# Second block's gate tiles by 2x2 blocks, its convolution summed in PSUM

## The chip, the cores and the metric

One NeuronCore of one Trainium2 chip runs the whole program. The metric is the device time of one execution in microseconds, the median of several runs.

## The reference, cut to what matters

Two blocks on 1024 tokens of width 1024, in float32. The first block is a state-space branch, a sparse attention branch, a merge and a gated feed-forward; it ends in a normalisation. The second block, which the change mostly touches:

```python
h = rmsnorm(x, norm_g); p = h @ w_in                      # 1024 x 8200 columns
gates = sigmoid(p[:, :3072] + b_gate)                     # g_a, g_b, g_c
a = a_in[:, :512] * sigmoid(a_in[:, 512:])                # conformer branch
a = causal_depthwise_conv(a, conv_w, conv_b)              # 31 taps, 512 channels
y_a = (silu(layernorm(a)) * silu(a_z)) @ w_a
y_b = (u * (tril(w_s) @ rmsnorm(v) + b_s) * silu(b_z)) @ w_b   # spatial branch
y_c = (attention(q, k, v, forget gates) * silu(c_z)) @ w_c     # 8 heads of 64
out = x + (g_a * y_a + g_b * y_b + g_c * y_c) @ w_out
```

The feed-forward of the first block is `(silu(u2 @ w_gate) * (u2 @ w_up)) @ w_down` with 2816 hidden columns (22 tiles of 128).

## The kernel before, in words

Activations lie transposed: 128 channels on the partitions, 1024 tokens along a row, eight such tiles for a width of 1024. Each float32 operand is kept as a rounded high half and a remainder, and a product is three matmuls (`mm3`): high x high, high x low, low x high. The halves are made by ScalarE (the cast, L130) and VectorE or GpSimd (the subtraction, L122). `linear` takes a weight 128 output columns at a time: 8 row tiles x 3 passes x 2 token halves = 48 matmuls of 512 columns, after which the caller's `evict` reads PSUM.

`wino` computes a pair of 128-column tiles on both token halves as a 2x2 by 2x2 block product with 7 products in place of 8; each product is 4 row tiles x 3 passes of 512 columns. It needs four sums of weight blocks per pair (`wino_weights`: GpSimd adds, then halves are made) and four sums of activation blocks once (`x4`, tiles `xth`, `xtl`). The weights of the next pair are asked for before the products of the present one. Before the change only the feed-forward uses it: hidden tiles 0 and 1 (pair 0) are computed plainly, and pairs 1 to 10 of gate and up by blocks.

All tiles are placed by a framework that adds the semaphores, hands out SBUF and PSUM, and orders each engine's instructions by a list scheduler with a time model; a manual dependency (`later`, and the third argument of `load`) only orders the schedule. Nearly all DMAs go through SyncE's queue, in order. `self.aside` is a generator of side work; `linear` and `linear_t` take one step of it after each output tile, and `together` sets how many steps that is.

In the order of the program: conditioning rows (`mod_setup`, then `mod_steps`: for each of parts 2, 3 and 4 VectorE sums 8 weighted rows of 1024, and TensorE turns the sum with 8 one-column matmuls directly behind the last row), projections of the first block, state-space branch, sparse attention, `merge1`, `out1` (with part 5 of the conditioning), `ffn`. Then the second block: `conv_in` (inputs of the convolution), `fox` (attention inputs, with `c_z`), `gmlp` (spatial branch), branch b with its 8 gate tiles, `conformer_gate` (`a_z`), the 8 gate tiles of branch c to DRAM, branch a with its 8 gate tiles, attention (`attend`), branch c, `out2`. Beside `fox`, `gmlp` and branch b run `keep_x2` and `conformer`: the convolution, 31 taps per channel tile, even ones on VectorE into an SBUF sum over 1024 tokens (`cx`, L125), odd ones as a ScalarE product and a GpSimd addition (`cy`, L122).

Of the kernel before, what the change touches and what calls it, by code (L numbers as in the profile page):

```python
# [17 lines left out]
T = 1024  # L18
# [50 lines left out]
class Core:  # L69
# [186 lines left out]
    def wino_weights(self, w, c0, kt=8, r0=0):  # L256

        gp, n = self.nc.gpsimd, kt // 2
        raw = self.sb.tile([128, 2 * T], F32, name="wq", tag="wq", bufs=2)[:, :256 * kt].rearrange("p (k n) -> p k n", n=256)
        for k in range(0, kt, n):  # L260
            self.load(raw[:, k:k + n],
                      w[r0 + k * 128:r0 + (k + n) * 128, c0:c0 + 256].rearrange("(k p) n -> p k n", p=128), self.tick)
        a11, a12 = raw[:, :n, :128], raw[:, n:, :128]
        a21, a22 = raw[:, :n, 128:], raw[:, n:, 128:]

        def parts(src, m):
            hi, lo = (blocks(self.pg(t, F32R, bufs=b)[:, :128 * m]) for t, b in (("vh", 4), ("vl", 4)))
            self.split(hi, lo, src)
            return hi, lo
        out = {}  # L270
        h, l = parts(raw[:, :, :128], kt)
        out["a11"], out["a12"] = (h[:, :n], l[:, :n]), (h[:, n:], l[:, n:])
        for name, bufs in (("s12", 1), ("s34", 1)):
            s = blocks(self.pg(name, bufs=bufs)[:, :128 * kt])
            if name == "s12":
                s2, s1 = s[:, :n], s[:, n:]
                self.tt(s1, a21, a22, OP.add, gp)
# [4 lines left out]
            h, l = parts(s, kt)  # L282
# [3 lines left out]
        out["a22"] = parts(a22, n)  # L286
        return out

    def wino(self, jobs, x, weights):
# [10 lines left out]
        def snap(p):  # L300
            if not spare:
                page = blocks(self.pg("snap", bufs=3), 512)
# [5 lines left out]
        for j, (_, evict) in enumerate(jobs):  # L308
# [18 lines left out]
            evict(1, 1, r, u3)  # L327

            def rest(a=a, evict=evict, p=p, r=r, u2=u2):
# [3 lines left out]
                evict(1, 0, p, None)  # L333
        rest()
# [158 lines left out]
    def mod_steps(self, parts):  # L493

        rows = [(part, k) for part in parts for k in range(8)]
        for n in range(0, len(rows), 2):
            for part, k in rows[n:n + 2]:
                w = self.pg("wmod", bufs=4)
                self.load(w, self.mod_rows(part, k), self.pace)
                if k == 0:  # L500
                    acc = self.pg("macc2", bufs=2)
                    self.ts(acc, w, self.cond[:, 0:1])
                else:
                    self.stt(acc, w, self.cond[:, k:k + 1], acc, OP.mult, OP.add)
            yield
            if k == 7:
                p = self.p1()
                for j in range(8):
                    self.mm(p[:, j:j + 1], acc[:, j * 128:(j + 1) * 128], self.ones[:, 0:1])
                self.mod[part] = self.small([8])  # L510
                self.tt(self.mod[part], p[:, 0:8], self.v["b_mod"][:, part * 8:part * 8 + 8], OP.add)
# [604 lines left out]
    def glu(self):  # L1116
# [16 lines left out]
        def ev(m, p):  # L1133
# [7 lines left out]
            self.load(tg, self.tg[i])  # L1141
# [187 lines left out]
    def merge1(self):  # L1329

        w = self.I["w_attn_proj"][0]
        self.mods = self.mod_steps([5])
# [3 lines left out]
        for s in range(2):  # L1336
            c = slice(512 * s, 512 * s + 512)

            def ev(m, p):
# [10 lines left out]
                if s == 1 and m % 2 == 1:  # L1350
# [16 lines left out]
    def out1(self):  # L1367
# [4 lines left out]
        self.stt(gs, self.mod[4], 1.0, self.v["norm2_g"], OP.add, OP.mult)  # L1372
# [12 lines left out]
        def norm(s):  # L1385
            c = slice(512 * s, 512 * s + 512)
            r = self.rsqrt_cols(self.col_sums(acc, half=s), D)
            yield
# [8 lines left out]
            for k in range(4) if s else ():  # L1397
                lo, hi = blocks(self.h[k], 512), blocks(self.h[k + 4], 512)
                b = sh[:, k + 4:k + 5]
                pages = [blocks(self.pg("tq", bufs=3), 512) for _ in range(2)]  # L1400
                (t1, t2), (t3, t4) = ((p[:, 0], p[:, 1]) for p in pages)
                self.tt(t1, lo[:, 1], lo[:, 0], OP.subtract, self.nc.gpsimd)
# [10 lines left out]
        for s in range(2):  # L1413
            c = slice(512 * s, 512 * s + 512)

            def ev(m, p):
# [13 lines left out]
                if s == 0 and m == 1:  # L1430
                    next(self.mods, None)
# [8 lines left out]
    def ffn(self, uh, ul, x4, norm):  # L1440
# [9 lines left out]
        for s in range(2):  # L1450
            c = slice(512 * s, 512 * s + 512)
            th = blocks(self.pg("f_th", bufs=3), 512)

            def ev_g(m, p):
                self.act(th[:, m], p, AF.Tanh, scale=0.5)
                self.stt(th[:, m], th[:, m], 1.0, p, OP.add, OP.mult)
                next(norm, None)

            def ev_u(m, p):
                self.tt(th[:, m], th[:, m], p, OP.mult)  # L1460
                next(norm, None)
            self.linear(wg, cols[:2], 8, uh, ul, ev_g, half=s)
            if s == 1:
                first = self.wino_weights(wg, 256)
            self.linear(wu, cols[:2], 8, uh, ul, ev_u, half=s)
            self.load(fd[0:2, :, c].rearrange("m p t -> p m t"), th)
# [3 lines left out]
        for pair in range(1, 11):  # L1470
# [55 lines left out]
        hl = self.sides("ul", 8)  # L1526
        self.r1 = [None, None]

        def norm(s):
# [10 lines left out]
            for k in range(8):  # L1540
                t = self.pg("sqn", bufs=2)[:, :512]
                self.stt(t, self.h[k][:, c], gg[:, k:k + 1], rb, OP.mult, OP.mult)
                self.split(hh[s][k], hl[s][k], t, eng=self.nc.gpsimd if k % 2 else None)
        norms = [norm(0), norm(1)]
        for s in range(2):
            c = slice(512 * s, 512 * s + 512)

            def ev_last(m, p):
# [3 lines left out]
                self.add_squares(acc2, h, m, fg[:, m:m + 1], half=s)  # L1552
                if s == 1 and m in (1, 3):
# [4 lines left out]
        return hh, hl, norms[1]  # L1558

    def keep_x2(self):  # L1560
# [3 lines left out]
        for k in range(8):  # L1564
            self.ts(self.h[k], self.h[k], fg[:, k:k + 1])
            o = blocks(self.pg("xc", bufs=2))
            for s in range(2):
                q = blocks(self.p1())
                for i in range(4):
                    self.tp(q[:, i], self.h[k][:, (4 * s + i) * 128:(4 * s + i + 1) * 128])  # L1570
# [5 lines left out]
    def fox(self, hh, hl):  # L1576
# [49 lines left out]
        self.fd = self.dram([4, 4, 2, 128, T], "fd")  # L1626
# [58 lines left out]
        for g in range(2):  # L1685
            def ev_v(i, p):
# [4 lines left out]
                self.split(hi, lo, flat(p))  # L1691
# [7 lines left out]
        def ev_z(m, p):  # L1699
            advance()  # L1700
            sz = self.pg("xraw", bufs=5)
            self.mark = self.act(sz, p, AF.Tanh, scale=0.5)
            self.stt(sz, sz, 1.0, p, OP.add, OP.mult)
            self.ts(sz, sz, 0.5, eng=nc.gpsimd)
            self.load(self.fd[m, 3, 0], sz)
        self.linear(w, [(7680 + 128 * t, 128) for t in range(4)], 8, hh, hl, ev_z)
# [59 lines left out]
    def gate(self, hh, hl, j, m, dst):  # L1766
        def ev(_, p):
            self.mark = self.act(dst, p, AF.Tanh, scale=0.5, bias=self.hbg[:, 8 * j + m:8 * j + m + 1])
        self.linear(self.I["w_in_2"][0], [(1024 * j + 128 * m, 128)], 8, hh, hl, ev)

    def branch(self, src, scale, wname, j, hh=None, hl=None):

        w = self.I[wname][0]
        if src is None:
            xh, xl = self.xh, self.xl
# [6 lines left out]
        for m in range(8):  # L1782
            th = self.pg("g_th", bufs=2)
            if hh is None:
                self.load(th, self.gtd[m], self.mark2)
            else:
                self.gate(hh, hl, j, m, th)

            def ev_y(_, p):
                if self.mg[m] is None:  # L1790
                    self.mg[m] = self.pg("mg", bufs=8)
                    self.stt(self.mg[m], th, 1.0, p, OP.add, OP.mult)
                else:
                    self.stt(th, th, 1.0, p, OP.add, OP.mult)
                    self.tt(self.mg[m], self.mg[m], th, OP.add, self.nc.gpsimd)
                if hh is None:
# [5 lines left out]
    def gmlp(self, hh, hl):  # L1802
        nc, I = self.nc, self.I
        w = I["w_in_2"][0]

        ws = self.pg("diag")
        self.load(blocks(ws[:, :512]), I["w_s_2"][0].rearrange("g t s -> t g s"), self.mark)
# [4 lines left out]
        for g in range(4):  # L1812
# [4 lines left out]
                  self.mark)  # L1817
# [49 lines left out]
    def conv_in(self, hh, hl, norm):  # L1867
        w = self.I["w_in_2"][0]
        self.ca = [self.pg("ca", bufs=4) for _ in range(4)]
        self.pace = self.tick  # L1870

        def part(t0, half):
# [7 lines left out]
            def ev_a(m, p):  # L1880
                x = self.ca[t0 + m][:, c]
                self.stt(x, x, 1.0, p, OP.add, OP.mult)
            for c0, ev in ((3584, ev_g), (3072, ev_a)):
# [4 lines left out]

    def conformer(self):

        gp = self.nc.gpsimd
        cw = self.small([31, 4])
        self.ts(cw, blocks(self.v["conv_w_2"], 4), 0.5)
        x = []
        for t in range(4):
            at = self.ca[t]
            y = self.pg("cx", bufs=4)

            self.ts(y, at, cw[:, 30, t:t + 1], self.v["conv_b_2"][:, t:t + 1], OP.mult, OP.add)
            y2 = self.pg("cy", bufs=2)  # L1900
            self.later(gp.memset(y2[:, 0:1], 0.0), self.pace)
            for k in range(29, -1, -1):
                s = 30 - k
                wk = cw[:, k, t:t + 1]
                if k % 2 == 0:
                    i = self.stt(y[:, s:], at[:, :T - s], wk, y[:, s:], OP.mult, OP.add)
                elif s == 1:
                    i = self.act(y2[:, 1:], at[:, :T - 1], scale=wk)
                else:
                    z = self.pg("ct", bufs=2)  # L1910
                    i = self.act(z[:, s:], at[:, :T - s], scale=wk)
                    self.tt(y2[:, s:], y2[:, s:], z[:, s:], OP.add, gp)
                self.later(i, self.pace)
                if k % 4 == 0:
                    yield
            self.tt(y, y, y2, OP.add)
            x.append(y)
            if t == 1:
                total = self.pg("sqa", bufs=4)
            if t > 0:  # L1920
# [157 lines left out]
```

## Time and profile before

| | |
|---|---|
| median of 3 runs | 2697.72 us (2697.37 to 2699.09) |
| the profiled execution | 2699.37 us, span 2697.31 us |
| mean granted TensorE clock | 0.977 |
| TensorE, VectorE, ScalarE, GpSimd busy | 95%, 59%, 41%, 37% |
| second block | from about 1600 us on |

Engines in the rows: PE is TensorE's matmuls, PEld its weight loads, DVE VectorE, ACT ScalarE, POOL GpSimd, SP SyncE; a "q" is an engine's instruction queue. Tiles are named `out<-in`: `wh`, `wl` are a weight's halves, `vh`, `vl` those of a block weight, `uh`, `ul` those of the activations, `pw`, `pl`, `p` PSUM tiles. L159 is every matmul, L135 every load.

### The profile page before, as it was taken

Reading aid. Unit: us, or ns where it says so; the run is one execution under the profiler, and the core shown is the slowest. Engines: PE = TensorE matmul, PEld = TensorE weight load, DVE = VectorE, ACT = ScalarE, POOL = GpSimd, SP = SyncE. Lnnn points to the kernel's source line nnn. Section 1 sums busy time; section 2 is a strip of 40 time slices with the busy share of each in tenths; the row PEclk is TensorE's granted clock in tenths of the full one; section 3 lists DMA queues with packets and bytes.
Section 4 is the critical chain, followed back from the end, with each engine's and each line's share of the span. In section 5 each row is a group of like instructions: output and inputs, shape, how many; then the busy total and the mean of one; then the engine's idle time right before and its main releaser. Section 6 shows DMA issues by size and latency. Waiting matters only on the chain.

```text
span 2697.3 us, 34931 instructions
## 1 busy us (share of the span) xinstructions
PE 2556.0 (95%) x12969; PEld 2152.9 (80%) x12969; DVE 1590.6 (59%) x2626; ACT 1099.2 (41%) x2056; POOL 1011.2 (37%) x931
## 2 busy tenths in 40 slices
PE   6989988896899999999999999999999999999999
PEld 4867877775788778888888888998987888888877
DVE  6753477969884764444453375457589621228871
ACT  6223358685953433333332243344434322118730
POOL 2777642265610264444300031237566210115530
PEclk9989999997999999999999999999999999999999
DMA  7554453464365322222452223344011213238632
GB/s 249 154 196 146 127 153 116 144 208 101 87 231 168 117 67 82 87 86 69 178 182 71 71 87 117 110 157 139 26 39 47 63 36 98 63 84 195 168 115 89
DMA packets 269305, 318.40 MB, mean 118 GB/s; under 512 B 42860, under 2 KB 219704, under 8 KB 269136
## 3 DMA queue, kind: packets, MB, share of 16 engines
q1 hardware_dynamic: 267760, 314.94, 37.9%
q0 software_dynamic: 1152, 1.21, 0.3%
q8 instruction: 102, 1.67, 0.2%
q14 instruction: 67, 0.55, 0.1%
q10 hardware_dynamic: 224, 0.03, 0.0%
HBM read 240.63 MB, written 73.40 MB: 116 GB/s over the span
## 4 chain that ended last, share of the span: by engine, by line
PE 54%; DVE 4%; issue 3%; POOL 2%; DMA 1%; ACT 1%; SPq 0%; DVEq 0%; POOLq 0%; ACTq 0%
PE pl L159 26%; PE pw L159 14%; PE p L159 12%; PE p L167 1%; DVE wl L122 1%; POOL cy L122 1%; DVE cx L125 1%; POOL gv L119 0%; DMA f_th<-fd 0%; DVE bb L122 0%; DMA fvs<-fd 0%; DMA kl<-fd 0%; DVE h L119 0%; DMA wr<-in_w_out_dram 0%; DVE bb L125 0%
## 5 line engine op out<-in xcount | busy, mean ns | idle before, releaser
L159 PE MATMUL pl<-uh,wl 128*128 128x512 f32 x1056 | 415.3, 394 | 6.6 <-DVE wl L122 3.8
L159 PE MATMUL pl<-uh,wh 128*128 128x512 f32 x1056 | 416.2, 395 | 1.7 <-ACT uh L132 1.1
L159 PE MATMUL pl<-ul,wh 128*128 128x512 f32 x1056 | 414.0, 392 | 0.0
L122 DVE TENSOR_TENSOR wl<-wr,wh 128x512 fp32r<-128x512 f32 (+1 forms) x292 | 243.6, 865 | 112.5 <-ACT wh L130 107.7
L130 ACT CAST wh<-wr 128x512 fp32r<-128x512 f32 x340 | 188.3, 596 | 212.5 <-PE pl L159 120.0
L159 PEld LDWEIGHTS pl<-uh,wl 128*128 128x128 f32 x1056 | 199.9, 189 | 49.4 <-DVE wl L122 5.2
L159 PEld LDWEIGHTS pl<-uh,wh 128*128 128x128 f32 x1056 | 200.3, 190 | 42.7 <-ACT uh L132 1.6
L159 PEld LDWEIGHTS pl<-ul,wh 128*128 128x128 f32 x1056 | 200.0, 189 | 41.1 <-DVE ul L125 0.3
L122 POOL TENSOR_TENSOR cy<-cy,ct 128x1021 f32<-128x1021 f32 (+13 forms) x56 | 159.2, 2843 | 79.2 <-ACT ct L132 76.6
L122 POOL TENSOR_TENSOR sqa<-sqa,sqn 128x512 f32<-128x512 f32 (+1 forms) x19 | 29.5, 1568 | 342.7 <-ACT sqn L132 342.7
L159 PE MATMUL p<-wth,uh 128*128 128x256 f32 x512 | 146.1, 286 | 0.0
L159 PE MATMUL p<-wtl,uh 128*128 128x256 f32 x512 | 144.8, 283 | 0.0
L159 PE MATMUL p<-wth,ul 128*128 128x256 f32 x512 | 144.8, 283 | 0.0
L122 DVE TENSOR_TENSOR snap<-pw,snap 128x512 f32<-128x512 f32 x60 | 41.2, 690 | 162.5 <-PE pw L159 87.3
L125 DVE SCALAR_TENSOR_TENSOR cx<-ca,small,cx 128x1022 f32<-128x1022 f32 (+14 forms) x60 | 131.2, 2186 | 1.0
L119 POOL TENSOR_SCALAR L<-L,small 128x128 f32<-128x128 f32 (+7 forms) x128 | 97.9, 771 | 85.6 <-DVE small L1173 80.6
L122 POOL TENSOR_TENSOR mg<-mg,g_th 128x1024 f32<-128x1024 f32 x16 | 47.2, 2955 | 218.1 <-DVE g_th L125 204.5
L159 PE MATMUL pw<-xtl,vh 128*128 128x512 f32 x320 | 124.5, 389 | 0.0
L159 PE MATMUL pw<-xth,vh 128*128 128x512 f32 x320 | 123.7, 389 | 0.0
L159 PE MATMUL pw<-xth,vl 128*128 128x512 f32 x320 | 123.5, 389 | 0.0
L122 POOL TENSOR_TENSOR wl<-wr,wh 128x512 fp32r<-128x512 f32 x48 | 64.5, 1357 | 128.9 <-ACT wh L130 50.9
L122 POOL TENSOR_TENSOR s<-wq 128x512 f32<-128x512 f32 x40 | 59.7, 1494 | 141.0 <-DMA wq<-in_w_ffn_gate_dram 53.6
(443 smaller groups left out, 6966.7 us busy)
## 6 DMA issues: line engine op xcount, KB each, us to landing
wr<-in_w_in_dram SPq DMA_DIRECT2D x64, 512.0 KB, 4.9
wmod<-in_w_mod_dram SPq DMA_DIRECT2D x48, 512.0 KB, 6.8
wr<-in_w_in_dram SPq DMA_DIRECT2D x67, 256.0 KB, 3.2
wr<-in_w_out_dram SPq DMA_DIRECT2D x24, 512.0 KB, 5.5
fd<-f_th SPq DMA_DIRECT2D x22, 512.0 KB, 4.3
f_th<-fd SPq DMA_DIRECT2D x22, 512.0 KB, 5.5
wq<-in_w_ffn_gate_dram SPq DMA_DIRECT2D x20, 512.0 KB, 5.4
wq<-in_w_ffn_up_dram SPq DMA_DIRECT2D x20, 512.0 KB, 4.9
```

The source lines that it names most:

```text
L119: return (eng or self.nc.vector).tensor_scalar(out=out, in0=a, scalar1=s1, scalar2=s2, op0=op0, **kw)
L122: return (eng or self.nc.vector).tensor_tensor(out=out, in0=a, in1=b, op=op)
L125: return self.nc.vector.scalar_tensor_tensor(out=out, in0=a, scalar=s, in1=b, op0=op0, op1=op1)
L130: return self.nc.scalar.copy(out, a)
L159: self.tick = self.nc.tensor.matmul(out, a, b, start=start, stop=stop, skip_group_check=True)
L167: return self.nc.tensor.transpose(out, a, self.ident[:n, :n])
```

## The change

The 24 gate tiles of the second block go through `wino` and to DRAM (`gates2`); the branches only read them back. Pair 1 of the feed-forward becomes plain. The gates `a_z` and `c_z` are computed ahead of the gate stage and kept in DRAM (`plain_gates`), the normalised stream is kept in DRAM (`hd2`) and reloaded by `keep_x2`, and four upper operand tiles go to DRAM over the gate stage (`upper`, `upper_back`). The convolution sums in PSUM, 512 tokens at a time: channel tiles 0 and 1 beside the gate stage with all taps on VectorE, tiles 2 and 3 beside `fox` with the odd taps on ScalarE and GpSimd as before. Part 4 of the conditioning moves from the first projections to `merge1` and `out1`, and each sum is turned three steps behind its last rows. Some GpSimd work goes to VectorE or ScalarE.

```diff
 def wino_weights(self, w, c0, kt=8, r0=0, ref=None):
-    raw = self.sb.tile([128, 2 * T], F32, name="wq", tag="wq", bufs=2)...
+    raw = [self.pg("wq", bufs=3)... for _ in range(2)]
 def wino(...):                       # snap pages 3 -> 2
     evict(1, 1, r, u3)
+    next(self.aside, None)
...
     evict(1, 0, p, None)
+    next(self.aside, None)
 def mod_steps(self, parts):
-    for n in range(0, len(rows), 2):
+    for n in range(0, len(rows) + 6, 2):
...
+        if n >= 12 and n % 8 == 4:
+            turn(parts[n // 8 - 1])
         yield
-        if k == 7: ...               # 8 matmuls, the sum's turn
-self.aside = self.together((self.mod_steps(range(2, 5)), 1.5))
+self.aside = self.together((self.mod_steps((2, 3)), 1.9))
 def merge1(self):
-    self.mods = self.mod_steps([5])  # a step at s == 1 and m % 2 == 1
+    self.mods = self.mod_steps((4, 5))   # at m % 4 == 3; in out1 at s == 0 and m < 7
 def out1(self):                      # operand sums of the first block
-    self.tt(t1, lo[:, 1], lo[:, 0], OP.subtract, self.nc.gpsimd)
+    self.tt(t1, lo[:, 1], lo[:, 0], OP.subtract)
-    self.split(th, tl, p, eng=self.nc.gpsimd if i else None)
+    self.split(th, tl, p)
 def ffn(...):
+    for pair in range(2):            # pairs 0 and 1 plain, in token halves
-    for pair in range(1, 11):
+    for pair in range(2, 11):        # by blocks
...
+    # norm(1): halves 0..3 of the upper operands to DRAM, then t1..t4 as in out1
 def gates2(self, x4, first):
+    for pair in range(12):
+        def ev(m, s, p, more, ...):
+            if more is not None:
+                self.tt(more, p, more, OP.add)
+            self.act(t, p if more is None else more, AF.Tanh, scale=0.5, bias=b)
+            if (m, s) in ((0, 1), (1, 0)):
+                self.load(self.gtd[2 * pair + m], g[m])
+        jobs.append((lambda pair=pair: self.wino_weights(w, 256 * pair), ev))
+    self.wino(jobs, x4, first)
 def conv(self, t, both):
+    taps = range(30, -1, -2 if both else -1)
+    for h in range(2):
+        acc = self.p1()
+        for n, k in enumerate(taps):
+            if s == 0:
+                i = self.ts(acc, at[:, c0:c0 + 512], wk, bias, OP.mult, OP.add)
+            else:
+                i = self.stt(acc[:, a:], at[...], wk, acc[:, a:], OP.mult, OP.add)
+            # both: two odd taps, ScalarE product and GpSimd addition, every second n
 def branch(self, src, scale, wname, j, last=False):
-    self.gate(hh, hl, j, m, th)      # branches a and b
+    self.load(th, self.gtd[8 * j + m], self.mark2 if last else self.pace)
-    self.tt(self.mg[m], self.mg[m], th, OP.add, self.nc.gpsimd)
+    self.tt(self.mg[m], self.mg[m], th, OP.add)
 def gmlp(self, hh, hl):
-    self.ts(x, x, r[:, i:i + 1], eng=nc.gpsimd)
+    self.act(x, x, scale=r[:, i:i + 1])
 def run(self):
     self.conv_in(hh, hl, norm)
+    first = self.plain_gates(hh, hl, norm)
+    self.aside = self.together(((None for t in range(2) for _ in self.conv(t, False)), 0.75))
+    self.gates2(x4, first)
+    self.upper_back(hh, hl)
+    self.spatial()
+    self.aside = ... conformer, conformer_gate, keep_x2, 1.3
     self.fox(hh, hl); self.gmlp(hh, hl)
-    self.branch(self.bb, 0.5, "w_b_2", 1, hh, hl)
+    self.branch(self.bb, 0.5, "w_b_2", 1)
-    self.conformer_gate(hh, hl); 8 gates of branch c to gtd
+    self.branch((self.abh, self.abl), None, "w_a_2", 0)
```

## Rows read from the trace of the kernel before

**Rows 1.** The page's first part: busy us, share of the span, instructions.
```profile
PE 2556.0 (95%) x12969; PEld 2152.9 (80%) x12969; DVE 1590.6 (59%) x2626; ACT 1099.2 (41%) x2056; POOL 1011.2 (37%) x931
```

**Rows 2.** Windows: stretch, length; us (count) of PE PEld DVE ACT POOL; clock; DMA.
```profile
160.00:180.00 20.00, 8.16 (x31) 7.34 (x30) 9.49 (x10) 2.54 (x4) 16.41 (x22) 0.58 0.73 224
810.00:855.00 45.00, 43.93 (x207) 36.30 (x206) 20.64 (x33) 15.29 (x27) 3.86 (x3) 0.96 0.51 167
905.00:958.00 53.00, 43.61 (x185) 34.07 (x183) 47.08 (x62) 23.47 (x36) 21.88 (x12) 0.97 0.24 76
...
1600.00:1690.00 90.00, 87.48 (x411) 73.02 (x412) 46.52 (x75) 25.00 (x45) 12.65 (x8) 0.98 0.29 88
1690.00:1840.00 150.00, 150.00 (x1250) 149.09 (x1249) 80.63 (x141) 56.77 (x82) 52.05 (x23) 1.00 0.48 152
1840.00:2047.00 207.00, 198.29 (x1075) 170.57 (x1074) 152.96 (x108) 76.70 (x116) 134.08 (x54) 0.99 0.18 50
...
2555.00:2593.00 38.00, 34.37 (x165) 28.00 (x165) 26.33 (x24) 14.29 (x21) 20.10 (x9) 1.00 0.31 109
```

**Rows 3.** The chain that ended last: start us, us, what.
```profile
966.84 369.03 PE pw L159 x1628
1338.88 9.12 DMA f_th<-fd
...
2133.64 287.11 PE pl L159 x1267
```

**Rows 4.** Timelines of SP, DVE and PE, 140 to 190: start, us, what [idle before].
```profile
146.59 0.33 SPq L135 DMA_DIRECT2D rot<-s_E  x1
...
160.72 1.24 SPq L135 DMA_DIRECT2D wmod<-in_w_mod_dram  x2
...
166.58 1.28 DVE L125 SCALAR_TENSOR_TENSOR macc<-wmod,small,macc 128x1024 f32<-128x1024 f32 x1 [21.16 <-DMA wmod<-in_w_mod_dram]
...
172.56 3.54 PE L159 MATMUL p<-small,macc 128*128 128x1 f32 x16 [11.84 <-DVE macc L125]
```

**Rows 5.** Timelines of POOL and DVE around 935, and of DVE at 1616.
```profile
935.38 2.38 POOL L122 TENSOR_TENSOR xtl<-tq,xth 128x1024 fp32r<-128x1024 f32 x1 [15.04 <-issue]
...
935.51 4.49 DVE L122 TENSOR_TENSOR wl<-wr,wh 128x512 fp32r<-128x512 f32 x2
...
1616.12 2.49 DVE L122 TENSOR_TENSOR wl<-wr,wh 128x512 fp32r<-128x512 f32 x4
```

**Rows 6.** Groups by shape, 966:1336, 1600:2430, page: busy, mean ns | idle.
```profile
L122 DVE TENSOR_TENSOR vl<-s,vh 128x1024 fp32r<-128x1024 f32 x39 | 50.8, 1302 | 24.4 <-ACT vh L130 15.4 <-POOL f_th L122 4.7 <-PE pw L159 2.3
L122 DVE TENSOR_TENSOR snap<-pw,snap 128x512 f32<-128x512 f32 x58 | 39.8, 690 | 156.1 <-PE pw L159 85.2 <-ACT snap L130 70.7
...
L122 DVE TENSOR_TENSOR vl<-wq,vh 128x512 fp32r<-128x512 f32 x20 | 20.4, 1022 | 1.9 <-PE pw L159 1.9
...
L122 POOL TENSOR_TENSOR s<-wq 128x512 f32<-128x512 f32 x38 | 56.2, 1482 | 141.0 <-DMA wq<-in_w_ffn_gate_dram 53.6 <-DMA wq<-in_w_ffn_up_dram 46.4 <-PE pw L159 22.0
...
L125 DVE SCALAR_TENSOR_TENSOR cx<-ca,small,cx 128x994 f32<-128x994 f32 x4 | 13.0, 3252 | 0.1
...
L125 DVE SCALAR_TENSOR_TENSOR ca<-ca,p 128x512 f32<-128x512 f32 x8 | 5.5, 684 | 20.3 <-PE p L159 20.3
...
L125 DVE SCALAR_TENSOR_TENSOR cx<-ca,small,cx 128x1022 f32<-128x1022 f32 x4 | 5.1, 1276 | 0.0
...
L122 POOL TENSOR_TENSOR cy<-cy,ct 128x1021 f32<-128x1021 f32 (+13 forms) x56 | 159.2, 2843 | 79.2 <-ACT ct L132 76.6
```

**Rows 7.** Waits of PE, 1330 to 1530: us, times, longest.
```profile
PE pl L159 <- DVE fl L122: 1.2, 1, 1.2
```

**Rows 8.** The chain at the end of the spatial branch: start us, us, what.
```profile
2041.45 2.87 DVE bb L122
...
2044.40 1.06 ACT atth L132
...
2045.49 1.24 DVE attl L125
```

More of the change, by code (lines that the diff above doesn't have):

```diff
@@ L495, in mod_steps, with turn @@
         rows = [(part, k) for part in parts for k in range(8)]
-        for n in range(0, len(rows), 2):
+        sums = {}
+        def turn(part):
+            p = self.p1()
+            for j in range(8):
+                self.mm(p[:, j:j + 1], sums[part][:, j * 128:(j + 1) * 128], self.ones[:, 0:1])
+            self.mod[part] = self.small([8])
+            self.tt(self.mod[part], p[:, 0:8], self.v["b_mod"][:, part * 8:part * 8 + 8], OP.add)
+        for n in range(0, len(rows) + 6, 2):
             for part, k in rows[n:n + 2]:
@@ L1451, in ffn, with ev_g, ev_u @@
             c = slice(512 * s, 512 * s + 512)
[L1452 to L1466, printed above, removed]
+            for pair in range(2):
+                th = blocks(self.pg("f_th", bufs=3), 512)
+                def ev_g(m, p):
+                    self.act(th[:, m], p, AF.Tanh, scale=0.5)
+                    self.stt(th[:, m], th[:, m], 1.0, p, OP.add, OP.mult)
+                    next(norm, None)
+                def ev_u(m, p):
+                    self.tt(th[:, m], th[:, m], p, OP.mult)
+                    next(norm, None)
+                two = cols[2 * pair:2 * pair + 2]
+                self.linear(wg, two, 8, uh, ul, ev_g, half=s)
+                if s == 1 and pair == 1:
+                    first = self.wino_weights(wg, 512, ref=self.tick)
+                self.linear(wu, two, 8, uh, ul, ev_u, half=s)
+                self.load(fd[2 * pair:2 * pair + 2, :, c].rearrange("m p t -> p m t"), th)
         for _ in norm:
@@ L1526, in ffn @@
         hl = self.sides("ul", 8)
+        self.hd2 = self.dram([8, 128, T], "hd2")
+        self.upper = self.dram([2, 4, 128, 512], "upper")
+        x4 = {"t1": [], "t2": [], "t3": [], "t4": []}
+        for name, s, ks in (("b11", 0, range(4)), ("b21", 0, range(4, 8)), ("b22", 1, range(4, 8))):
+            x4[name] = [(hh[s][k], hl[s][k]) for k in ks]
         self.r1 = [None, None]
@@ L1708, in fox_heads, with upper_back @@
+    def upper_back(self, hh, hl):
+        for i, (x, tag) in enumerate(((hh, "uh"), (hl, "ul"))):
+            for k in (0, 2):
+                p = blocks(self.pg(tag, bufs=8), 512)
+                self.load(p, self.upper[i, k:k + 2].rearrange("k p t -> p k t"), self.pace)
+                p = p.bitcast(F32R)
+                x[1][k], x[1][k + 1] = p[:, 0], p[:, 1]
     def fox_heads(self):
@@ L1764, in fox_heads, with branch @@
         yield
[L1766 to L1771, printed above, removed]
+    def branch(self, src, scale, wname, j, last=False):
         w = self.I[wname][0]
-        if src is None:
-            xh, xl = self.xh, self.xl
+        if isinstance(src, tuple):
+            xh, xl = src
         else:
@@ L1882, in ev_a @@
                 self.stt(x, x, 1.0, p, OP.add, OP.mult)
+                if half == 1:
+                    self.load(self.cad[t0 + m], self.ca[t0 + m])
             for c0, ev in ((3584, ev_g), (3072, ev_a)):
@@ L1889, in conformer @@
     def conformer(self):
         gp = self.nc.gpsimd
[L1892 to L1920, printed above, removed]
-                self.tt(total, x[0] if t == 1 else total, y, OP.add, gp)
-            self.show(f"conv{t}", y)
@@ L1923, in conformer @@
+        yield from self.conv(2, True)
+        x = self.cx
+        for t in range(2):
+            x[t] = self.pg("cx", bufs=4)
+            self.load(x[t], self.cyd[t], self.pace)
+        yield from self.conv(3, True)
+        total = self.pg("sqa", bufs=4)
+        self.tt(total, x[0], x[1], OP.add, gp)
+        yield
+        self.tt(total, total, x[2], OP.add, gp)
+        self.tt(total, total, x[3], OP.add)
+        yield
         mean = self.small([8])
```

238 lines of the change are left out of this document (165 added, 73 removed).

## The prediction

> **What bounds the kernel now.** I read the page first: TensorE is busy for 95% of the span, VectorE for 59% [rows 1]. Then the windows by stage, to see which stage has slack on the engines that the change loads [rows 2]. Then the chain of waits, because a busy share of modelled matmuls is no rate: the first block's 2x2-block stage puts 1628 matmuls of 512 columns into 369.03 us, and the second block's gate tiles put 1267 into 287.11 us [rows 3]. Both are 0.2267 us each, so both stages run at one rate without a gap, and a matmul fewer there is 0.2267 us less. Last, what the windows leave idle of TensorE, and what stands on the timeline and the chain there.
>
> The kernel is bound by the number of matmuls in most stages, and by late operands at four places: 11.8 us of 20 at 160 to 180, 53 - 43.61 = 9.4 us before the 2x2-block stage of the first block, 207 - 198.29 = 8.7 us in the spatial branch, 38 - 34.37 = 3.6 us in the last branch [rows 2].
>
> **The change part by part.** The profiled execution took 2699.37 us with a span of 2697.31 us; the median of the runs shown is 2697.72 us, 1.65 us lower. The sum is a difference, so I take it from the median.
>
> *Gate tiles.* A pair of tiles of 128 columns takes 2 x 48 = 96 matmuls plainly, and 7 products x 4 row tiles x 3 passes = 84 by blocks. 12 pairs save 144 x 0.2267 = 32.6 us.
>
> *First block, pair 1.* Gate and up of one pair go back to the plain form: 2 x 12 = 24 matmuls more, +5.4 us. So TensorE's own sum is -27.2 us.
>
> *Conditioning steps.* At 160 to 172 TensorE stood 11.84 us, since its column sums stood in its queue before the last two rows of the weight had been multiplied; VectorE had waited 21.16 us for that load, and the load had gone out at 160.72, behind a table store that SyncE's queue could only pass at 146.59 [rows 4]. The window's granted clock was 0.58, so the stop also ran what followed at 1.2 GHz for part of it [rows 2]. The change asks for the sums three steps behind the last rows, makes more steps per tile (1.9 for 1.5), and takes 8 of the 24 loads out of this stage. It may still meet the same blocked queue: bounds 0 and -14 (the wait and some 2 us of low clock); I take -8. The steps that move go into the two merge stages: 8 rows of 1.28 us on VectorE [rows 4], and 8 loads of 512 KB. In the out-projection's first half VectorE is busy 20.64 of 45 us and DMA at 0.51 [rows 2], so they are covered; were they not, 4 steps x 1.28 x 2 = 10 us. I take 0.
>
> *Start of the first block's 2x2 stage.* From 905 to 958 VectorE is busy 47.08 of 53 us [rows 2], and TensorE stands for 9.4. One reason is in the rows: four weight subtractions of 512 columns take 2.49 us undisturbed, 0.62 each, and two took 4.49 us while GpSimd ran a subtraction of its own from 935.38 [rows 5]. The change moves GpSimd's part to VectorE and has twice the plain tiles (16 half tiles of 24 x 0.2267 = 5.4 us, 87 us) over it. VectorE's work there: the normalisation 16 x 0.68 = 10.9, the operand sums 4 x (0.62 + 3 x 0.68 + 2 x 1.24) = 20.6 (1024 columns taken as twice 512), and weights and evictions 16 x (1.24 + 0.68) = 31: 62 of 87 us. It can bunch in the first half (47 of 43.5 us). Bounds +4 and -10; I take -6.
>
> The Trainium skill (SBUF — State Buffer, Who interferes with whom) says that a VectorE instruction with two SBUF inputs and a GpSimd instruction that reads SBUF take turns at a shared port, and one with at most one SBUF input does not. By that rule all 9.4 us should go, and the sum would be -41.6; the trace agrees in kind, the 4.49 us beside 2 x 0.62, but the bunching is left, and the sum keeps -6.
>
> *Second normalisation and operand sums.* The same work, in the convolution's input stage: VectorE is busy 46.52 of 90 us [rows 2]. What is added is 4 subtractions of 0.62 and 20.6 us of sums, spread over the sixteen half tiles and the first whole ones; what goes is the scaling of the kept activations. Covered; without cover, 3 us. I take 0.
>
> *Inside the gate stage.* New beside 12 x 84 x 0.2267 = 228.5 us of matmuls: VectorE makes five halves per pair (1.30 twice, 1.02 three times at most) and adds three snapshots (0.69 each), 7.7 us, x 12 = 92 us [rows 6]; and the convolution of two channel tiles, 31 taps x 2 halves x 2 = 124 instructions that add 512 columns into PSUM. No row before writes PSUM from VectorE. From below, a 512-column instruction with one PSUM operand is 0.68 us; from above, the present tap of 994 columns in SBUF is 3.25 us beside GpSimd, 1.68 us per 512 columns [rows 6]. At 0.68 the tap work is 84 us and VectorE is busy 176 of 228 us; at 1.68 it is 208 and VectorE needs 300. I take 0.68, the nearest row: same length, one PSUM operand. GpSimd has only 5.8 us per pair of sums there (4 x 1.48) [rows 6]. ScalarE's copies and halves are half a pair's time, as in the first block, where this stage shows no wait. Late operands: +2.
>
> *Into and out of the gate stage.* The block weights are made two tiles (21.8 us) ahead; on leaving, the next projection needs its first weights and the 8 upper operands back from DRAM, with memory that the last products free. The like passage in the first block has a 9.12 us load on the chain [rows 3], of which 1.2 us was left as a wait for its lower half [rows 7]. I take +4, bounds 1 and 13.
>
> *Attention inputs.* Half of the convolution runs beside them: 64 taps x 0.68 = 44 us on VectorE, which is busy 80.63 of 150 us, without the kept rows, and 28 additions of 2.8 us [rows 6] = 80 us on GpSimd, which is busy 52.05 us, some of these additions among it: 132 of 150 us at most [rows 2]. TensorE has no wait there now. One of the four PSUM banks is held by the sum. +2, bounds 0 and 17 (below).
>
> *Spatial branch.* GpSimd is busy 134.08 of 207 us and VectorE 152.96 [rows 2]; the 8.7 us stand behind taps of up to 3.25 us [rows 6] and a product of 2.87 us [rows 8]. Half of the taps are gone, the others mostly done, and the scaling goes from GpSimd to ScalarE. I take -7, bounds 0 and -8.7.
>
> *Branches without gates.* 16 tiles of 24 x 0.2267 = 5.4 us replace tiles of 16.3. VectorE needs 0.62 + 1.24 + 1.24 = 3.1 us per tile. What lacks cover is the start: the last product of the spatial branch, 2.87 at most, its rounding, 1.06, and its lower half, 1.24 [rows 8], stood under a gate tile of 10.9 us; now only three row tiles, 9 matmuls, 2.0 us, go ahead of it: +3. In the last branch the addition moves from GpSimd to VectorE: of the 3.6 us, -1.
>
> Sum: -32.6 + 5.4 - 8 - 6 + 0 + 0 + 2 + 4 + 2 - 7 + 3 - 1 = -38.2 us; 2697.7 - 38.2 = 2659.5, so 2660 us.
>
> **The rivals.**
> *The matmuls alone* (chance 0.23): the waits move rather than go. TensorE's -27.2 us are sure once the stage runs at its rate; the conditioning load stays behind the blocked queue (0), VectorE bunches before the first 2x2 stage (0), the spatial branch keeps half (-4), and entries and starts cost 13: 2697.7 - 27.2 - 4 + 13 = 2680. For it: a wait removed here was one of several late operands. Against: the rows name the cause of two of them.
> *VectorE becomes the bound of the gate stage* (0.08): the place is the 124 PSUM taps. It decides from 92 + 124 t = 228, t = 1.10 us. At 1.68 the stage takes 300 us, +72 on the forecast: 2732, slower. At 1.28, +23: 2683. For it: reading and writing one PSUM range in place, instruction upon instruction, stands in no row. Against: the present taps are in place too, and run at 1.28 us for 1022 columns when undisturbed [rows 6].
> *GpSimd holds the attention inputs* (0.09): GpSimd has up to 132 of 150 us there. A weight half of VectorE that has to wait for one 2.8 us addition in each of the 6 groups costs 17 us: 2677. For it: the present taps, which run beside those additions, go from 1.28 to 3.25 us. Against: the stage had its first additions already, and TensorE stood for nothing.
>
> The rule of the Trainium skill named above is what would do it; the price is worked out from the addition's row.
> *All waits go* (0.12): -27.2 - 14 - 9.4 - 8.7 - 2, and +7 for the new passages: 2643. For it: each has a named cause that the change touches. Against: four things must go right at once.
> *No change to speak of* (0.04): entries and exits each wait for a whole load chain, twice 13 us: 2697.
>
> **How the numbers follow.** The forecast has 0.44, 2650 to 2670. 2660 is its time. The range of 2640 to 2688 takes in the matmuls alone, GpSimd's and the good case, and leaves out VectorE's bound and the rest, 0.15 or so. This measurement tells apart 0.2%, 5.4 us. Slower by more than that: the larger part of VectorE's rival and mishaps, 0.08. Within: 0.05. Faster: 0.87.
>
> **What would show it.** Right: block products of the gates at 0.227 us each, 1008 of them, in under 235 us; taps near 0.68 us; no 11.8 us wait for the conditioning sums; under 5 us of waits before the first 2x2 stage. Wrong: VectorE at nine tenths in the gate stage; TensorE waiting for weight halves beside GpSimd's additions in the attention inputs; waits over 10 us where the gate stage begins or ends.

## The result, and the profile after

The changed kernel takes 2614.59 us, median of 4 runs (2612.61 to 2621.87), beside 2698.40 us for the kernel before; the ratio is 0.9692, 95% interval [0.9672, 0.9713]. That is 83.8 us less; the forecast was 38 less, 2660 us, with a range that ended at 2640. The profiled execution took 2621.87 us with a span of 2620.2 us, so of the 83.8 us the two traces place 77.1; the rest is the distance of this execution to its median and is not placed.

The first part of the page; against [rows 1] TensorE has 120 matmul records less, GpSimd 163 us less to do, VectorE 63 us more.

```profile
PE 2515.9 (96%) x12849; PEld 2119.9 (81%) x12849; DVE 1653.9 (63%) x2882; ACT 1129.7 (43%) x2144; POOL 847.9 (32%) x889
```

Windows of the second block, columns as in [rows 2]: the convolution's input, the gate stage, attention inputs, spatial branch, last branch. The length less PE's busy time is what TensorE stood.

```profile
1541.00:1633.00 92.00, 90.27 (x406) 74.01 (x405) 62.50 (x98) 37.76 (x63) 5.69 (x4) 1.00 0.42 139
...
1720.00:1954.00 234.00, 234.00 (x1056) 194.81 (x1055) 165.14 (x217) 97.56 (x148) 63.41 (x46) 1.00 0.39 128
...
1973.00:2155.00 182.00, 172.20 (x1425) 171.40 (x1424) 116.89 (x175) 80.27 (x131) 101.30 (x43) 0.98 0.34 109
2155.00:2267.00 112.00, 106.87 (x520) 89.88 (x519) 71.14 (x95) 34.33 (x48) 4.77 (x2) 0.97 0.31 94
...
2475.00:2528.00 53.00, 51.82 (x260) 43.48 (x259) 40.41 (x50) 25.45 (x38) 7.58 (x8) 1.00 0.51 189
```

VectorE's groups by shape in and around the gate stage (1715 to 1960): busy us, mean ns of one. The first row is the operation that no row of before showed, a tap that adds 512 columns into PSUM: 0.752 us.

```profile
L125 DVE SCALAR_TENSOR_TENSOR p<-ca,small,p 128x512 f32<-128x512 f32 x60 | 45.1, 752 | 1.2
L122 DVE TENSOR_TENSOR vl<-s,vh 128x1024 fp32r<-128x1024 f32 x22 | 32.2, 1462 | 3.2 <-ACT vh L130 3.0
L122 DVE TENSOR_TENSOR snap<-pw,snap 128x512 f32<-128x512 f32 x36 | 24.8, 690 | 53.8 <-PE pw L159 34.5 <-ACT snap L130 18.9
L122 DVE TENSOR_TENSOR vl<-wq,vh 128x512 fp32r<-128x512 f32 x33 | 21.8, 685 | 1.3 <-ACT vh L130 1.3
```

What TensorE waited for in the attention inputs (us in all, times, longest), and, in the second fence, before the 2x2 stage of the first block, where [rows 2] had 9.4 us:

```profile
PE p L167 <- POOL xraw L122: 5.3, 1, 5.3
PE p L159 <- DVE xsl L125: 3.1, 1, 3.1
PE pl L167 <- DVE small L125: 1.4, 1, 1.4
```

```profile
PE p L159 <- DVE wl L122: 1.4, 1, 1.4
PE p L159 <- ACT wh L130: 0.5, 1, 0.5
```

**Where the time came from.** Two marks cut the program: the merge's first matmul (`p<-atth,wh`) and the second block's first.

| stretch | before | after | difference | forecast |
|---|---|---|---|---|
| start to merge | 759.3 | 712.0 | -47.3 | -8 |
| merge to second block | 829.1 | 829.1 | 0.0 | -0.6 |
| second block | 1108.9 | 1079.1 | -29.8 | -29.6 |

So the large edits came out as forecast, and what was missed lies ahead of the merge, where the diff has only the conditioning steps and one line in `glu`, the output stage of the state-space branch: `self.load(tg, self.tg[i], self.pace)`. It is not among the lines of the change shown above, and the prediction did not price it at all. Ahead of the merge TensorE stood for 104.5 us before and for 66.9 after, and was busy for 9.7 us less, at a mean granted clock of 0.93 before and 0.96 after:

```profile
0.00:759.30 759.30, 654.77 (x3399) 547.40 (x3400) 537.65 (x1213) 418.30 (x936) 402.25 (x521) 0.93 0.49 151
...
0.00:712.00 712.00, 645.10 (x3382) 536.01 (x3383) 534.91 (x1203) 418.04 (x935) 394.07 (x521) 0.96 0.50 156
```

**What ends the stretch before the merge.** Three groups of the timeline by tile, for the kernel before: the state-space branch's products (`s_d`), the keys with which the threshold search of the sparse attention begins (`tk_l`; there are six), and the masks it ends with (`mb`). Each row: minimum, median and longest in ns, then the start of the first and of the last. The last row is the early load of `tg`.

```profile
L159 PE MATMUL p<-s_d,s_O x128: 269/275/582, 293.5 to 457.3; 128*128 128x127 f32 x128
...
L119 DVE TENSOR_SCALAR tk_l<-sc x6: 415/602/1426, 262.8 to 371.0; 128x384 int32<-128x384 int32 x1, 128x512 int32<-128x512 int32 x1, 128x640 int32<-128x640 int32 x1, 128x768 int32<-128x768 int32 x1
...
L119 DVE TENSOR_SCALAR mb<-tk_eq x5: 293/395/2458, 604.3 to 641.2; 128x512 bf16<-128x512 bf16 x1, 128x640 bf16<-128x640 bf16 x1, 128x768 bf16<-128x768 bf16 x1, 128x896 bf16<-128x896 bf16 x1
...
L135 SPq DMA_DIRECT2D g_tg<-tg x2: 338/338/338, 248.3 to 265.9; - x2
```

The same of the changed kernel; its first two `tg` loads go out at 462.59 and 481.37.

```profile
L159 PE MATMUL p<-s_d,s_O x128: 269/275/578, 240.4 to 430.2; 128*128 128x127 f32 x128
...
L119 DVE TENSOR_SCALAR tk_l<-sc x6: 369/586/1248, 272.8 to 289.7; 128x384 int32<-128x384 int32 x1, 128x512 int32<-128x512 int32 x1, 128x640 int32<-128x640 int32 x1, 128x768 int32<-128x768 int32 x1
...
L119 DVE TENSOR_SCALAR mb<-tk_eq x5: 362/733/1514, 521.1 to 556.6; 128x512 bf16<-128x512 bf16 x1, 128x640 bf16<-128x640 bf16 x1, 128x768 bf16<-128x768 bf16 x1, 128x896 bf16<-128x896 bf16 x1
...
462.59 0.39 SPq L135 DMA_DIRECT2D g_tg<-tg  x1
481.37 0.46 SPq L135 DMA_DIRECT2D g_tg<-tg  x1
```

Before, the sixth key came at 371.0 and the last mask at 641.2. VectorE reads the attention's logits out of PSUM only behind their masks, and TensorE stood for it. TensorE's timeline of the kernel before, idle time in brackets, and its window:

```profile
606.34 0.44 PE L159 MATMUL pl<-akh,aqq 128*128 128x384 f32 x1 [3.85 <-DVE small L1169]
618.07 0.80 PE L159 MATMUL pl<-akh,aqq 128*128 128x512 f32 x1 [7.67 <-DVE small L1169]
...
640.72 1.75 PE L167 MATMUL p<-small,L 128*128 128x128 f32 x7 [5.21 <-POOL L L119]
```

```profile
600.00:650.00 50.00, 25.30 (x92) 20.55 (x91) 48.03 (x89) 18.01 (x38) 18.99 (x24) 0.64 0.50 125
```

TensorE is busy half of that window, at a granted clock of 0.64: part of it ran at 1.2 GHz, with VectorE full. After, the window from 600 to 700 is

```profile
600.00:700.00 100.00, 94.37 (x660) 83.45 (x659) 89.02 (x258) 90.74 (x221) 66.81 (x115) 0.98 0.40 96
```

### The profile page after: what moved, and what is told of

The parts are those of the page before. It is cut to its first block, busy times and chain, and to the rows that moved or that the text cites. A ratio compares the mean times of both kernels' runs of the same rounds, so it can differ in the third digit from the quotient of the medians.

```text
span 2620.2 us, 35143 instructions
## 1 busy us (share of the span) xinstructions
PE 2515.9 (96%) x12849; PEld 2119.9 (81%) x12849; DVE 1653.9 (63%) x2882; ACT 1129.7 (43%) x2144; POOL 847.9 (32%) x889
## 5 line engine op out<-in xcount | busy, mean ns | idle before, releaser
L130 ACT CAST wh<-wr 128x512 fp32r<-128x512 f32 (+1 forms) x308 | 170.7, 594 | 325.1 <-PE pl L159 125.9
L159 PE MATMUL pl<-uh,wh 128*128 128x512 f32 x672 | 266.6, 397 | 1.1 <-ACT uh L132 1.1
L159 PE MATMUL pl<-uh,wl 128*128 128x512 f32 x672 | 264.6, 394 | 0.6 <-DVE wl L122 0.6
L159 PE MATMUL pl<-ul,wh 128*128 128x512 f32 x672 | 263.9, 393 | 0.0
L159 PEld LDWEIGHTS pl<-uh,wl 128*128 128x128 f32 x672 | 127.8, 190 | 27.7 <-DVE wl L122 1.1
L159 PEld LDWEIGHTS pl<-uh,wh 128*128 128x128 f32 x672 | 127.6, 190 | 26.9 <-ACT uh L132 1.2
L159 PEld LDWEIGHTS pl<-ul,wh 128*128 128x128 f32 x672 | 127.9, 190 | 26.2 <-DVE ul L125 0.5
L159 PE MATMUL pw<-uh,vh 128*128 128x512 f32 x360 | 140.0, 389 | 0.0
L159 PE MATMUL pw<-ul,vh 128*128 128x512 f32 x360 | 140.0, 389 | 0.0
L159 PE MATMUL pw<-uh,vl 128*128 128x512 f32 x360 | 136.6, 389 | 0.0
```

The costliest lines, as they stand in the source:

```text
L130: return self.nc.scalar.copy(out, a)
L159: self.tick = self.nc.tensor.matmul(out, a, b, start=start, stop=stop, skip_group_check=True)
```

## The experiments

Differences to the changed kernel are between ratios to the kernel before on the same chip, times 2698 us; each ratio's interval is about 0.002 to either side, so one such difference is known to some 7 us.

**Conditioning alone, and undone.** The first theory: the stretch ahead of the merge is the conditioning edits' work. They were put alone into the kernel before, and alone taken out of the changed one.

```diff
 # mod_steps, merge1, out1 and run as in the change; nothing else
-self.aside = self.together((self.mod_steps(range(2, 5)), 1.5))
+self.aside = self.together((self.mod_steps((2, 3)), 1.9))
```

> The kernel before with the conditioning edits alone (part 4 moved to the merge stages, each sum turned three steps late, 1.9 steps per tile). Theory: these edits carry nearly all of what the first block gained, 47 us at the first merge matmul (759.3 to 712.0): 2650 us (2645 to 2662), the threshold search's last counting pass at about 490 us in place of 557, TensorE not idle at the start of the sparse attention. Rival: the edits are worth the one stop of 11.8 us and some low clock, and the rest of the first block's gain comes with the other parts of the change (memory that they free, another order): 2684 to 2690 us, the search still ending near 557.

> The changed kernel with the conditioning as before (parts 2 to 4 in the first projections, turned at once, 1.5 steps per tile, part 5 in the merge). Theory: the first block loses its gain, 2614.6 + 45 = 2660 us (2648 to 2664). Rival: 2614.6 + 8 to 13 = 2623 to 2628 us.

Alone: 2710.23 us, ratio 1.0052 [1.0035, 1.0068], slower by 13 us; both the theory and its rival missed. Undone: 2638.06, ratio 0.9782 [0.9762, 0.9801], 24 us over the changed kernel, between the theories. The same edits cost time in one kernel and save it in the other. In the trace of the run alone, the state-space branch ended earlier than before, yet the last mask came later:

```profile
L159 PE MATMUL p<-s_d,s_O x128: 269/275/582, 240.1 to 448.8; 128*128 128x127 f32 x128
...
L119 DVE TENSOR_SCALAR mb<-tk_eq x5: 293/359/2454, 620.3 to 651.2; 128x512 bf16<-128x512 bf16 x1, 128x640 bf16<-128x640 bf16 x1, 128x768 bf16<-128x768 bf16 x1, 128x896 bf16<-128x896 bf16 x1
```

**Gate tiles plain, and pair 1 by blocks again.** To see whether the steps that looked right were right.

```diff
 def gates2(self, hh, hl):
+    self.linear(w, [(128 * m, 128) for m in range(24)], 8, hh, hl, ev)
-    self.wino(jobs, x4, first)
```

> The changed kernel with the 24 gate tiles computed plainly in the place of the block products, everything else kept (the operand sums for the blocks are made and not used). Theory: 144 matmuls more at 0.2267 us, +32.6 us, and nothing else moves: 2647 us (2643 to 2652). Rival: the block stage lets VectorE or its entries hold it up, so that less than the matmuls is lost by the plain form: +20 us or less, under 2637 us.

2650.48 us, ratio 0.9827 [0.9810, 0.9843]: 36 us over the changed kernel, as the count of matmuls says (32.6).

```diff
-for pair in range(2):      # plain pairs; by blocks from 2
+for pair in range(1):      # plain pair 0; by blocks from 1
```

> The changed kernel with pair 1 of the feed-forward by blocks again, so that the plain cover before the first 2x2-block stage is one pair as in the kernel before. Theory: 24 matmuls fewer, -5.4 us, but the waits for weight halves before the stage come back, +8 us: 2617 us (2612 to 2621), with 6 to 10 us of waits there. Rival: what removed the waits is the move of GpSimd's part to VectorE, and the cover was not needed: 2609 us, under 3 us of waits.

2620.08 us, ratio 0.9715 [0.9700, 0.9729]: 6 us over, inside what can be told, and the two profiled executions lie the other way round (spans of 2617.8 us here, 2620.2 in the changed kernel). Its trace has 4.4 us of waits before the 2x2 stage, not the 6 to 10 of the theory, beside 1.9 in the changed kernel and 9.4 before [rows 2]. So most of the waits went without the longer cover, and whether the 24 matmuls that the plain pair adds are paid back stays open.

**The `tg` line alone, and undone.** The second theory: the early `tg` loads hold two pages of SBUF over the search.

```diff
-self.load(tg, self.tg[i])
+self.load(tg, self.tg[i], self.pace)
```

> The kernel before with one line of the change: the load of the stored gate (g_tg) in the state-space branch's output stage is ordered behind the last output tile, and no longer free to go out as early as the schedule likes. Theory: that early load (248 and 266 us) holds two 4 KB pages for 270 us, the threshold search's last key then has no page until 371, and the sparse attention starts late; so this line alone brings the search's second step from 379 to about 285, its last counting pass from 556 to under 515, and 25 to 40 us: 2665 us (2655 to 2675). Rival: the load is off the path and the first block's gain belongs to the conditioning edits together with the memory that the rest of the change frees: 2690 us or more.

> The changed kernel with that one line as before (g_tg loads free to go early). Theory: the two loads go out near 265, the search's second step comes only at about 390, the sparse attention starts with TensorE idle, and the time is 2614.6 + 50 = 2665 us (2650 to 2675), as the kernel with the conditioning edits alone lost 57 us in the first block against the changed one. Rival: 2614 to 2622 us.

Alone 2680.21 us, ratio 0.9933 [0.9918, 0.9947], -18 us, less than the theory expected and more than the rival. Undone in the changed kernel 2671.71, ratio 0.9900 [0.9885, 0.9915], 56 us over it, as expected. With the line undone the key is late again, as in the kernel before:

```profile
L119 DVE TENSOR_SCALAR tk_l<-sc x6: 494/687/1495, 271.8 to 350.1; 128x384 int32<-128x384 int32 x1, 128x512 int32<-128x512 int32 x1, 128x640 int32<-128x640 int32 x1, 128x768 int32<-128x768 int32 x1
...
L119 DVE TENSOR_SCALAR mb<-tk_eq x5: 295/359/2459, 619.8 to 650.7; 128x512 bf16<-128x512 bf16 x1, 128x640 bf16<-128x640 bf16 x1, 128x768 bf16<-128x768 bf16 x1, 128x896 bf16<-128x896 bf16 x1
```

**Is it the room or the loads?** An early `tg` is two pages, but also two transfers, two places in SyncE's queue and two GpSimd instructions. So two pages, and then one, were held idle in the changed kernel, without the transfers; all that they add is a GpSimd memset and a VectorE read of one column for each page. `tg` itself stays late.

```diff
+self.hold2 = [self.pg("hold2", bufs=2) for _ in range(2)]   # 4 KB a partition each
+for x in self.hold2: nc.gpsimd.memset(x[:, 0:1], 0.0)
...
+    if i < 2:          # read once at the first gate tiles, then free
+        self.later(self.ts(keep[:, i:i + 1], self.hold2[i][:, 0:1], 1.0), self.mark)
```

> The changed kernel with two idle pages of 4 KB kept from the first gate tile of the projections until the first two gates of the output stage, so that SBUF has as little room as with the early loads, but no early load. Theory (room): the search's last key is late again and the time rises by 20 to 55 us, 2635 to 2670 us. Rival (the early loads hurt as transfers, in SyncE's queue or by their bandwidth): 2614 to 2622 us.

> The changed kernel, with one idle page of 4 KB a partition held from the first projections until the first gate tile of the first block; two such pages cost 71 us. If there is just no room to spare, one page costs some part of that: 2630 to 2670 us, with the sixth key of the search between 300 and 370 us. If there is a page to spare, 2611 to 2622. If any page held delays the last key alike, 2675 to 2690.

Two pages: 2685.46 us, ratio 0.9956 [0.9939, 0.9973], 71 us over, more than the 20 to 55 expected. One page: 2638.97, ratio 0.9770 [0.9755, 0.9784], 21 us over, as expected. Two pages held:

```profile
L692 POOL MEMSET hold<- x2: 102/102/102, 11.9 to 11.9; 128x1 f32 x2
L119 DVE TENSOR_SCALAR small<-hold x2: 144/146/148, 519.4 to 534.9; 128x1 f32<-128x1 f32 x2
...
L119 DVE TENSOR_SCALAR tk_l<-sc x6: 352/658/1443, 290.1 to 367.9; 128x384 int32<-128x384 int32 x1, 128x512 int32<-128x512 int32 x1, 128x640 int32<-128x640 int32 x1, 128x768 int32<-128x768 int32 x1
...
L119 DVE TENSOR_SCALAR mb<-tk_eq x5: 294/360/2452, 636.8 to 667.7; 128x512 bf16<-128x512 bf16 x1, 128x640 bf16<-128x640 bf16 x1, 128x768 bf16<-128x768 bf16 x1, 128x896 bf16<-128x896 bf16 x1
```

The pages are written at 11.9 us and read at 519.4 and 534.9, so they are held from long before the early loads take theirs (266.6 and 278.4 with the line undone), and the first key comes 18 us later than with the line undone. From the first key on the two runs are alike: 78 us to the sixth key in both, and 494 and 497 us to the merge, where the changed kernel takes 439. So behind the first key two pages, without the loads, cost what the early loads cost; that the whole is 71 us and not 56 fits the longer hold. The same memsets and reads on a small tile were not tried. Two kernels whose edits come only behind the merge, the plain gates and pair 1 by blocks, reach the merge at 710.8 and 712.2, the changed kernel at 712.0.

One page held: the sixth key comes 27 us later than in the changed kernel, and the state-space branch ends 17.5 us later.

```profile
L159 PE MATMUL p<-s_d,s_O x128: 269/275/578, 255.0 to 447.7; 128*128 128x127 f32 x128
...
L119 DVE TENSOR_SCALAR tk_l<-sc x6: 360/662/1511, 270.7 to 316.7; 128x384 int32<-128x384 int32 x1, 128x512 int32<-128x512 int32 x1, 128x640 int32<-128x640 int32 x1, 128x768 int32<-128x768 int32 x1
```

**Which part of the conditioning edits?** Part 3 moved as well; then, one at a time, the immediate turn, part 4 and the rate as they had been.

```diff
-self.aside = self.together((self.mod_steps((2, 3)), 1.9))
+self.aside = self.together((self.mod_steps((2,)), 1.9))         # part 3 to the merge
+self.aside = self.together((self.mod_steps((2, 3, 4)), 1.9))    # part 4 back
+self.aside = self.together((self.mod_steps((2, 3)), 1.5))       # rate as before
+if k == 7: ...                                                  # turn behind the last row
```

> The changed kernel with part 3 of the conditioning also moved from the first projections to the merge stages (part 2 alone stays). Theory: one part moved out is worth half of what both conditioning edits gave here (23.5 us), since the index scores stand behind the rows in VectorE's queue: 2604 us (2598 to 2612). Rival: no further gain, since the scores already start at 158, or a loss in the merge, whose window already has DMA at 0.84: 2615 to 2625 us.

2611.45 us, ratio 0.9676 [0.9660, 0.9692]: 4 us under the changed kernel, not to be told from it, so the further gain of the theory is not shown. In this run the merge also takes a conditioning step at every second tile, in place of every fourth.

> The changed kernel, with each conditioning sum turned directly behind its last rows again; part 4 stays in the merge, the rate stays 1.9. With all of the conditioning edits undone the kernel took 23.5 us more than the changed one. If the late turn carries that (TensorE no longer stands behind the sum, 11.8 us, and runs at 2.4 GHz behind it), this takes 2628 to 2642 us. If moving part 4 carries it (eight loads and eight rows less before the index scores), this takes 2612 to 2622.

2623.70 us, ratio 0.9714 [0.9700, 0.9729]: 6 us over, inside the noise; its trace reaches the merge at 711.4, as the changed kernel's at 712.0, and TensorE waits 2.0 us for a conditioning sum.

> The changed kernel, with part 4 of the conditioning back in the first projections (parts 2, 3 and 4 there, part 5 in the merge); the late turn and the rate of 1.9 stay. If moving part 4 carries the 23.5 us of the conditioning edits, 2628 to 2642 us and index scores from about 175 us on. If the late turn carries them, 2612 to 2622 and index scores from about 159 us on. Where both are needed, this and the run without the late turn both come out above 2625.

2649.28 us, ratio 0.9802 [0.9786, 0.9818]: 30 us over. The index scores start at 157.6, early, against the 175 expected where the move matters, but TensorE waits 20.8 us in them for ScalarE (`rel`), 4.3 in the changed kernel, and the state-space branch ends at 464.7, later than before. So of the conditioning edits it is mostly the move that pays. That this run is no better than the one with all of them undone fits the late turn's price in room, since a sum's page is then held three steps longer; this was not tried apart, and what the 20.8 us have to do with room is not shown.

> The changed kernel, with the conditioning steps taken at 1.5 per tile, as before, in place of 1.9; the late turn and the move of part 4 stay. If the rate is without effect, 2611 to 2619 us. If the steps must be through early (their pages are wanted by the search's keys), 2622 to 2650, with the sixth key of the threshold search later than 300 us.

2628.25 us, ratio 0.9732 [0.9717, 0.9746]: 11 us over, with the sixth key at 317.0: as the second theory has it.

**What the twelve runs have in common.** The starts fit two chains that race to the merge: the search's masks, and the state-space branch with the first block's gate tiles behind it. Starts of the last `s_d` product, the sixth key, the last mask and the merge, read from each trace by tile:

| kernel | last `s_d` | sixth key | last mask | merge | less mask | less `s_d` |
|---|---|---|---|---|---|---|
| before | 457.3 | 371.0 | 641.2 | 759.3 | 118.1 | 302.0 |
| conditioning alone | 448.8 | 350.9 | 651.2 | 769.1 | 117.9 | 320.3 |
| `tg` undone | 449.1 | 350.1 | 650.7 | 768.4 | 117.7 | 319.3 |
| two pages held | 466.6 | 367.9 | 667.7 | 784.4 | 116.7 | 317.8 |
| `tg` alone | 454.7 | 278.0 | 595.6 | 738.6 | 143.0 | 283.9 |
| conditioning undone | 448.2 | 273.7 | 588.9 | 730.8 | 141.9 | 282.6 |
| part 4 back | 464.7 | 321.0 | 593.5 | 746.7 | 153.2 | 282.0 |
| one page held | 447.7 | 316.7 | 582.8 | 734.3 | 151.5 | 286.6 |
| rate as before | 449.3 | 317.0 | 587.0 | 729.0 | 142.0 | 279.7 |
| after | 430.2 | 289.7 | 556.6 | 712.0 | 155.4 | 281.8 |

Where the key is late (350 or more), the merge starts 117 to 118 us after the last mask, whatever the state-space branch did. Where it is early, 280 to 287 us after the last `s_d` in this table, whatever the masks did. The four runs that the table leaves out lie at 278 to 284 after the last `s_d`. By it the numbers of both edits alone come out: before, the state-space chain was ready at 457.3 + 283 = 740 by this estimate, so freeing the masks alone could bring no more than 19 us, and it brought 20.7 at the merge; the conditioning edits alone brought that chain to 732, but the masks came 10 us later, and so did the merge. Only both together let the merge start at 712. The other parts of the change add less: 0.7 us at the merge between conditioning alone and `tg` undone, 7.8 between `tg` alone and conditioning undone. The rule was seen after the runs, and it is read from traces; which tile of the search waits for which page is in no row, and stays open. The kernel before with both edits and nothing else was not tried.

## Why the prediction was wrong

**The step that failed** is the conditioning steps' -8, with bounds 0 and -14, and with it the `tg` line at nothing. It priced the one wait that the rows named, 11.84 us [rows 4]. That wait was not the price: it is gone from the changed kernel, and with the turn immediate again but part 4 moved it is 2.0 us, and nothing is lost that can be measured. What the edits did, as the runs with held pages and with the old rate have it, is give pages back while the search starts: the early `tg` loads held two from 248 us on, and part 4's rows, loaded until 187 us, and its sum, turned at 266, some more before. That it is pages for the conditioning rows too is argued from these runs; no run holds pages in their place. Worth, in the changed kernel: 56 us for the `tg` line, 24 us for conditioning, and 47 for the whole change at the merge, not their sum, since each needs the other. The place to see it in the trace of before was there: a window of 50 us with TensorE half busy, and behind it a last mask whose key came at 371 where four of the six had come by 270 us. I had listed four places of late operands and not this one, the largest. Freed alone it is worth 19 us by the table, and it brought 20.7 at the merge; the rest is mostly the interaction, for which both chains had to be followed.

**Gate tiles, -32.6**: right; plain gates gave 36 back. The stage's 234 us show no wait and hold the 1008 block products and 48 narrower matmuls of the next stage, VectorE at 165 of 234 (176 of 228 forecast), a tap at 0.752 us (0.68 taken, 1.68 the upper bound). The rival of VectorE as the bound, which decided at 1.10 us a tap, is refuted. Inside the stage +2 was 0.

**Pair 1, +5.4, and the start of the 2x2 stage, -6**: right together. TensorE's waits there went from 9.4 us [rows 2] to 1.9, and to 4.4 without the longer cover, which is the smaller part; the merge to the second block took the same time.

**Into and out, +4, and attention inputs, +2**: 9.8 us of waits in 182, over one and a half times the sum. 5.3 of it is GpSimd's scaling of `xraw`, the third rival on a small scale and with another instruction than the addition that it named; GpSimd is busy 101 of 182 us.

**Spatial branch, -7**: the wait fell from 8.7 to 5.1 us, -3.6; a product that stood behind taps is gone, but `diag` on ScalarE is late by 4.1. **Branches, +3 and -1**: 0.9 us of wait in the first, and 3.6 to 1.2 in the last. All waits of these steps were forecast at +3 and came to about +5. That the second block as a whole came within 0.2 us of its sum is luck: single terms were off by up to 4 us, either way.

**The rivals**: the matmuls alone (2680) and no change (2697) are out. *All waits go*, 2643, came nearest in time, but not by its mechanism: the waits that it listed went only in part.

## What to carry to other kernels

Before pricing an edit by the wait that names it, list every window in which the bounding engine is idle, largest first, and follow each back to its chain: here the largest was not on the list. Where a scheduler places work by free memory, an early prefetch costs more than its transfer: count the pages that an edit takes and gives by stretch, as one counts instructions. And where two chains race, price edits together; one alone can cost what both would save.

## What the runs showed of the hardware

A tap of VectorE that sums in PSUM took as long with GpSimd busy beside it as without: four of 512 columns took 3.12 us, 0.78 each, while GpSimd was busy, and three took 2.32, 0.77 each, while it was idle. The last row is the next instruction of GpSimd, with the idle time before it in brackets.

```profile
2013.22 3.77 POOL L122 TENSOR_TENSOR xraw<-xraw,small 128x1024 f32<-128x1024 f32 x2 [1.77 <-issue]
2014.26 3.12 DVE L125 SCALAR_TENSOR_TENSOR p<-ca,small,p 128x512 f32<-128x512 f32 x4
...
2107.48 2.32 DVE L125 SCALAR_TENSOR_TENSOR p<-ca,small,p 128x512 f32<-128x512 f32 x3
2110.76 2.42 POOL L122 TENSOR_TENSOR wtl<-wr,wth 128x1024 fp32r<-128x1024 f32 x1 [10.72 <-DMA fd<-xsl]
```

A tap in SBUF had taken 1276 ns for 1022 columns, and 3252 for 994 beside GpSimd [rows 6]. Per 512 columns 3252 ns is 1675, so with its sum in PSUM a tap beside GpSimd takes less than half of that. The Trainium skill (SBUF — State Buffer, Who interferes with whom) says that a VectorE instruction contends with a GpSimd instruction that reads SBUF if it has two inputs in SBUF or runs in a two-port mode. A tap that sums in PSUM has one, beside its weight of one column, and these rows agree. GpSimd's side shows little: its four additions of a pair took 5.7 us beside the PSUM taps and 5.8 in the first block before.
